# One S5 block and its SwiGLU on one core: the factor products as sums, and the first halves of the last two units ahead of the late part

## The chip, the cores and the metric

The program runs on one core of a Trainium2 chip. The core has a matrix engine (TensorE, here PE, with its weight loads PEld), a vector engine (VectorE, DVE), a scalar engine (ScalarE, ACT), a general engine (GpSimd, POOL) and a queue processor (SyncE, SP). Each takes its instructions in the order in which they are written, and waits on semaphores of the others. DMA transfers are issued by SP, ACT or POOL and run beside the engines. The metric is the time of one execution in microseconds (us) on the device.

## The reference

The function is one layer of a backbone on 1024 latent tokens and 256 context tokens with 1024 channels: a bidirectional S5 mixer (64 groups of 16 channels, 64 complex states each, two directions, the latent scan starting from the final context state), a GELU and a gated linear unit, then a SwiGLU with 2816 hidden channels. All inputs and outputs are float32.

```python
def s5_direction(u_ctx, u_lat, lam_re, lam_im, log_step, b_re, b_im, c_re, c_im):
    lam = lax.complex(lam_re.astype(F32), lam_im.astype(F32))
    lam_bar = jnp.exp(lam * jnp.exp(log_step.astype(F32))[:, None])
    b_bar = ((lam_bar - 1.0) / lam)[..., None] * lax.complex(b_re.astype(F32), b_im.astype(F32))
    ...
        _, h = lax.associative_scan(_linear_combine, (a, bu), axis=0)
        return jnp.einsum('lgn,ghn->lgh', h, c_mat).real, h[-1]
...
    def out(y, h):
        y = y.reshape(h.shape).astype(h.dtype) + d_skip * h
        g = jax.nn.gelu(y)
        return g * jax.nn.sigmoid(g @ w_glu + b_glu)
...
        x = x + m_l[2][:, None] * y_l
        h_l = modulate(rms_norm(x, norm_ffn[i]), m_l[3][:, None], m_l[4][:, None])
        x = x + m_l[5][:, None] * swiglu(h_l, ffn_w1[i], ffn_w3[i], ffn_w2[i])
    return rms_norm(x, norm_final)
```

## The kernel before, in words

**Blocks of eight steps.** The 1024 latent tokens are 128 columns of T = 8 steps. The state is scanned on DVE from column to column (`scan()`, about 97 us in one piece), for all groups and both directions at once, in a tile `STE` in RA (its quarters `STQ[0]` to `STQ[3]`). What a column adds to the output is then two products on PE: the states at its edge times a matrix `CL` (powers of lambda times C), and the block's own inputs times a Toeplitz matrix of the kernel values.

**Units.** The 64 groups are worked off as eight units of 8 groups, 0 to 7; two units share a quarter q = unit // 2 of `CL`. The columns of a unit are made in two halves, as the scan reaches the middle first: `states_mm(k, ..., 0, ...)` multiplies the first half's states into two PSUM banks and `x_mm` adds the Toeplitz product of all columns; ACT copies that to `Y`. After the scan the late half follows, and DVE adds it to `Y`. Since the second direction runs backwards, its states are copied in reversed order first (`turned`).

**Two strings set the order.** `PROG1` and `PROG2` list operations that `run` emits one by one on all engines; each engine keeps that order. A letter names the operation, its digits the unit, quarter or part:

- A: matmuls of the modulation (weights loaded by SP); M0 copies their sums out and frees a buffer. G, L, q, n: sign, load and sums for `CL`'s factors.
- C: the products of `CL` for quarter q (C20 to C23 for q = 2), five steps per direction: three products on POOL (`prod`) and two adds. `HOWS` says of each add where it runs: P on PE (two matmuls with the identity, then an ACT copy), Y as a DMA that accumulates into its target, issued by POOL (L696), E as an add on POOL.
- K: the kernel values of a unit on PE (L842 to L850), copied out of PSUM by ACT and written to DRAM (`kd`, L854 and L855). T: a Toeplitz matrix read back from `kd` by SP (L863); unit k needs T(2k) and T(2k+1), which take buffer number (index mod 4) in RA.
- R: the reversed first-half states, on ACT (L955). P: first half and transform of a unit on PE (L975, L999). Y: copies of its two banks to `Y` on ACT (L1057). F: fills of the odd columns on POOL.
- Z, N, D: reversed late states, late half on PE (L975) and its add on DVE (L1063). z, Q: for units 6 and 7 alone, reversed states of all columns, then on PE transform (L999) and states of all columns (`states_all`, L988). H: GELU on ACT, for units 6 and 7 straight from PSUM (L1069), else in place (L1066).
- I, J: transposes of four steps of a unit on PE (L1123), high parts on ACT and low parts on DVE. w, l, b, m: loads by SP. W, V: the gate's weight rounded (L1080) and its rest (V1, on POOL and DVE). x: a factor on `Y` on POOL. g: matmuls of the gated unit (L1163, L1164); g03 is token step 0 with units 0 to 3, g05 the same with unit 4 and 5. The other matmuls of that unit begin at L1175.

The first string runs while DVE scans. In the second one PE is fed by N, I, Q and g; then come the rest of the gated unit and the SwiGLU, which take the remaining three quarters of the time and aren't touched. Each T waits for all writes of its `kd` and for its buffer; each Y copy frees a PSUM bank; the late part takes its banks from the same eight.

Of the kernel before, what the change touches and what calls it, by code (L numbers as in the profile page):

```python
# [13 lines left out]
AF = mybir.ActivationFunctionType  # L14
# [3 lines left out]
P = 128  # L18
# [11 lines left out]
HOWS = "YPYP EPEP YEYE YPYE"  # L30
ZEN = "VVSVSVSV"
PROG1 = ("A22 G1 B0 A26 A30 C01 O0 C03 q1 A34 K0 O1 A38 A42 C10 C11 K1 O2 L2 A46 A50 C12 C13 A54 K2 O3 A58 T0 T1 T2 T3 F10 F11 G2 R0 K3 L3 R1 P0 Y0 Y1 A64 M0 P1 T4 T5 R2 Y2 Y3 G3 q2 C20 T6 T7 C21 P2 R3 Y4 Y5 C22 M1 P3 Y6 Y7 C23 q3 C30 K4 K5 R4 T8 T9 T10 T11 C31 C32 C33 F30 F31 P4 R5 Y8 Y9 K6 P5 Y10 Y11 K7 T12 T13 T14 T15 w0 l1 M2 m0 w1")
PROG2 = ("Z0 N0 Z1 Z2 D0 Z3 N1 D1 Z4 H0 H1 N2 D2 H2 N3 Z5 D3 H3 N4 D4 z6 z7 I0 J0 I1 J1 H4 N5 D5 I2 J2 H5 I3 J3 W0 W1 W2 W3 x0 x1 x2 x3 Q6 H6 I4 J4 Q7 I5 J5 V1 b0 w20 w21 l1 H7 g03 g13 I6 J6 g23 g05 g15 I7 J7 V2 g26 x10 x11 x12 x13")
# [9 lines left out]
def s5_ffn_kernel(tc, a, out):  # L43
# [3 lines left out]
    with ctx:  # L47
# [572 lines left out]
        def pw_sums(i):  # L620

            gs = slice(16 * i, 16 * i + 16)
            tt(PS[i], PWF[:, :, 0, :, gs], PWF[:, :, 1, :, gs], ADD, E)
            if i == 0:
                tt(PWF[:, :, 1, :, gs], PWF[:, :, 1, :, gs], PWF[:, :, 0, :, gs], SUB, E)
            else:
                for d, gs, neg in ((slice(0, 2), slice(16, 24), True), (slice(0, 1), slice(24, 32), False), (slice(1, 2), slice(24, 32), True)):
                    re, im = PWF[:, :, 0, d, gs], PWF[:, :, 1, d, gs]
                    tt(im, re if neg else im, im if neg else re, SUB, E)
# [49 lines left out]
        def cl_ops(q, d):  # L679
# [8 lines left out]
            def add(o, how, last):  # L688
                if how == "P":
                    for h in range(2):  # L690
# [3 lines left out]
                        S.activation(o[:, hs].rearrange("p g t h -> p (g t h)"), pc, AF.Copy, scale=-1.0 if last else 1.0)  # L694
                elif how == "Y":
                    E.dma_start(o, ct, accum_op=ADD)  # L696
# [1153 lines left out]
```

## Time and profile before

| what | value |
| --- | --- |
| three runs | 1011.56, 1005.89, 1008.38 us, median 1008.38 |
| profiled execution | 1006.91 us, span 1005.1 us, mean granted clock 0.984 |
| ACT busy | 427.7 us (43%) |
| DVE busy | 774.3 us (77%) |
| HBM read, written | 83.20 MB, 6.17 MB |

How to read it: the span is the time from the first to the last instruction of the profile, the execution has some microseconds around it. A row of a timeline gives the start, the busy time of the group, the engine, the line, the operation, target<-sources by the program's names, their shape (partitions x elements) and count; in square brackets is the idle time before it and what ended it. PE records two passes for a float32 matmul, so 32 matmuls of the program are 64 records. A trailing q on an engine's name means that it issues a DMA. `c` is a tile of `CL`, `pw`, `pm` and `kt` are PSUM banks of the first string, `pe` those of the second.

### The profile page before, as it was taken

The page shows a single profiled execution, that of the slowest core. Times are in us where ns is not written, and L with a number is a line of the kernel's source. Part 1 is how long each engine was busy: PE and PEld are TensorE (multiplying, and loading weights), DVE is VectorE, ACT ScalarE, POOL GpSimd, SP SyncE. Part 2 cuts the span into 40 slices and gives each one's busy share as a digit, 9 for nine tenths or more (in the row PEclk, how much of TensorE's full clock was granted, in tenths as well). Part 3 has the DMA queues.
Part 4 walks back from the last instruction along what each step waited for, and adds up shares of the span by engine and source line. Part 5 has one row for each costly group of instructions (what it writes and reads, how often), then busy time and mean ns, then how long its engine had stood idle before and what let it go on. Part 6 is the DMA issues. An engine that isn't in the chain of part 4 may idle for free. (4 is left out here: it accounts for less than half of the span.)

```text
span 1005.1 us, 17726 instructions
## 1 busy us (share of the span) xinstructions
PE 952.8 (95%) x6604; PEld 751.5 (75%) x6604; DVE 774.3 (77%) x1630; ACT 427.7 (43%) x808; POOL 748.7 (74%) x595
## 2 busy tenths in 40 slices
PE   5987898879999999999999999999999999999996
PEld 1466535769888778778888888888888888888885
DVE  7979899984556778878869586685958677686977
ACT  5478622224434563343233343434243343334337
POOL 5799998963734458979786869777785878777764
PEclk9999998889999999999999999999999999999999
DMA  9765998535520032011212121111212120111205
GB/s 335 285 133 108 287 316 273 125 85 171 210 64 22 1 105 84 11 43 42 74 53 74 42 79 34 47 61 45 74 42 84 43 64 32 61 55 53 74 22 167
DMA packets 49118, 99.95 MB, mean 99 GB/s; under 512 B 4348, under 2 KB 18940, under 8 KB 47752
## 3 DMA queue, kind: packets, MB, share of 16 engines
q1 hardware_dynamic: 43416, 86.64, 26.1%
q0 software_dynamic: 2592, 9.44, 5.1%
q10 hardware_dynamic: 3024, 2.74, 0.9%
q8 instruction: 52, 0.85, 0.3%
q14 instruction: 34, 0.28, 0.1%
HBM read 83.20 MB, written 6.17 MB: 89 GB/s over the span
## 5 line engine op out<-in xcount | busy, mean ns | idle before, releaser
L77 POOL TENSOR_TENSOR c<-rxc,c 128x512 fp32r<-128x512 f32 x127 | 166.0, 1320 | 52.3 <-ACT c L1305 51.5
L1364 PE MATMUL ut<-ra,c 128*128 128x512 f32 x400 | 155.7, 389 | 1.2 <-DVE ra L77 1.2
L1363 PE MATMUL ut<-ra,c 128*128 128x512 f32 x400 | 155.7, 389 | 0.2 <-ACT ra L1305 0.2
L1365 PE MATMUL ut<-ra,c 128*128 128x512 f32 x400 | 155.6, 389 | 0.0
L1305 ACT CAST c<-rxc 128x512 fp32r<-128x512 f32 x128 | 79.0, 622 | 147.6 <-PE xt L1658 53.0
L1658 PE MATMUL xt<-c,c 128*128 128x512 f32 x540 | 129.7, 389 | 0.0
L77 DVE TENSOR_TENSOR ru<-ru,xt 128x1024 f32<-128x1024 f32 x90 | 107.9, 1216 | 13.4 <-PE xt L1658 9.4
L1658 PEld LDWEIGHTS xt<-c,c 128*128 128x128 f32 x540 | 101.4, 188 | 21.0
L77 DVE TENSOR_TENSOR ru<-ut,ru 128x512 f32<-128x512 f32 x98 | 67.2, 686 | 44.1 <-PE ut L1365 38.6
L1364 PEld LDWEIGHTS ut<-ra,c 128*128 128x128 f32 x400 | 75.1, 188 | 17.1 <-POOL rxc L77 1.5
L1363 PEld LDWEIGHTS ut<-ra,c 128*128 128x128 f32 x400 | 75.1, 188 | 16.1 <-ACT ra L1305 0.6
L1365 PEld LDWEIGHTS ut<-ra,c 128*128 128x128 f32 x400 | 75.1, 188 | 15.6
L77 POOL TENSOR_TENSOR c<-ru,c 128x512 fp32r<-128x512 f32 (+1 forms) x39 | 58.8, 1507 | 10.1 <-ACT c L1305 5.7
L77 POOL TENSOR_TENSOR rxc<-rxc 128x512 f32<-128x512 f32 (+1 forms) x44 | 63.8, 1450 | 2.2 <-ACT rxc L671 0.6
L77 POOL TENSOR_TENSOR c<-rw,c 128x512 fp32r<-128x512 f32 (+1 forms) x28 | 37.4, 1337 | 37.5 <-ACT c L1305 37.5
L1363 PE MATMUL ut<-c,c 128*128 128x512 f32 x160 | 62.3, 390 | 0.8 <-DVE rxa L77 0.8
L1364 PE MATMUL ut<-c,c 128*128 128x512 f32 x160 | 62.3, 389 | 0.0
L1365 PE MATMUL ut<-c,c 128*128 128x512 f32 x160 | 62.2, 389 | 0.0
L1658 PE MATMUL ut<-c,c 128*128 128x512 f32 x216 | 51.9, 389 | 0.0
L77 DVE TENSOR_TENSOR ru<-ru,ut 128x512 f32<-128x512 f32 x76 | 47.3, 680 | 0.7 <-ACT ru L1712 0.5
L1658 PEld LDWEIGHTS ut<-c,c 128*128 128x128 f32 x216 | 40.5, 188 | 8.4
L587 PE MATMUL pv<-ru,c 128*64 128x160 f32 x512 | 41.4, 312 | 5.2 <-ACT c L450 2.0
(453 smaller groups left out, 2392.0 us busy)
## 6 DMA issues: line engine op xcount, KB each, us to landing
c<-in_ada_w SPq DMA_DIRECT2D x46, 256.0 KB, 5.9
rxc<-in_w SPq DMA_DIRECT2D x38, 256.0 KB, 2.9
rxc<-in_w SPq DMA_DIRECT2D x19, 512.0 KB
c<-c POOLq DMA_DIRECT2D x11, 512.0 KB, 5.7
ru<-in_w SPq DMA_DIRECT2D x11, 512.0 KB
rw<-in_w SPq DMA_DIRECT2D x11, 512.0 KB, 3.6
ra<-in_ada_w SPq DMA_DIRECT2D x10, 512.0 KB, 10.8
ra<-in_ada_w SPq DMA_DIRECT2D x18, 256.0 KB, 8.8
```

The lines of the kernel that those rows point to most:

```text
L77: eng.tensor_tensor(out=o, in0=x, in1=y, op=op)
L587: PE.matmul(pv[64 * (i % 2):64 * (i % 2) + 64, ri, c0:c0 + 160], w[:, i, 64 * ri:64 * ri + 64], U[:, 8 * b + 4 * j + i], start=True, stop= ...
L1305: S.copy(o[0], x)
L1363: PE.matmul(pu, wh, bh, start=start, stop=False)
L1364: PE.matmul(pu, wh, bl, start=False, stop=False)
L1365: PE.matmul(pu, wl, bh, start=False, stop=stop)
L1658: PE.matmul(pd, w[:, cs_], b, start=j in (1, 2, 4) and n == 0, stop=n == 2, skip_group_check=j not in (1, 2, 4))
```

## The change

Of the two adds per direction of `CL` the first was a sum and the second a difference or a negated sum, which only E and P can do. Now the factors carry the sign (`pw_sums` and `cs_sum`), so that every add is a plain sum; with that the adds of quarter 2 are all accumulating DMAs (before: two DMAs, two POOL adds), and of quarter 3 the second one (before on PE). The factor sums of quarters 2 and 3 (`pw_sums(1)`, now operation n1) are two POOL operations and one on ACT, ahead of F10, where q2 had four on POOL. A64 and M0 stand before P0 now.

Units 6 and 7 are worked like the others: R6, R7, S6, S7 (first halves), X6, X7 (transforms) and Y12 to Y15 end the first string, and the second one has Z6, Z7, N6, N7, D6, D7 for z6, z7, Q6, Q7. S7 and X7 use the banks `pw` and `pm`. K7 stands right behind K6 now and w0 between T13 and T14.

```diff
@@ -27,10 +27,10 @@
 NS = 64
 EPS = 1e-6
 MAGIC = 12582912.0
-HOWS = "YPYP EPEP YEYE YPYE"
+HOWS = "YPYP EPEP YYYY YYYE"
 ZEN = "VVSVSVSV"
-PROG1 = ("A22 G1 B0 A26 A30 C01 O0 C03 q1 A34 K0 O1 A38 A42 C10 C11 K1 O2 L2 A46 A50 C12 C13 A54 K2 O3 A58 T0 T1 T2 T3 F10 F11 G2 R0 K3 L3 R1 P0 Y0 Y1 A64 M0 P1 T4 T5 R2 Y2 Y3 G3 q2 C20 T6 T7 C21 P2 R3 Y4 Y5 C22 M1 P3 Y6 Y7 C23 q3 C30 K4 K5 R4 T8 T9 T10 T11 C31 C32 C33 F30 F31 P4 R5 Y8 Y9 K6 P5 Y10 Y11 K7 T12 T13 T14 T15 w0 l1 M2 m0 w1")
-PROG2 = ("Z0 N0 Z1 Z2 D0 Z3 N1 D1 Z4 H0 H1 N2 D2 H2 N3 Z5 D3 H3 N4 D4 z6 z7 I0 J0 I1 J1 H4 N5 D5 I2 J2 H5 I3 J3 W0 W1 W2 W3 x0 x1 x2 x3 Q6 H6 I4 J4 Q7 I5 J5 V1 b0 w20 w21 l1 H7 g03 g13 I6 J6 g23 g05 g15 I7 J7 V2 g26 x10 x11 x12 x13")
+PROG1 = ("A22 G1 B0 A26 A30 C01 O0 C03 q1 A34 K0 O1 A38 A42 C10 C11 K1 O2 L2 A46 A50 C12 C13 n1 A54 K2 O3 A58 T0 T1 T2 T3 F10 F11 G2 R0 K3 L3 R1 A64 M0 P0 Y0 Y1 P1 T4 T5 R2 Y2 Y3 G3 q2 C20 T6 T7 C21 P2 R3 Y4 Y5 C22 M1 P3 Y6 Y7 C23 q3 C30 K4 K5 R4 T8 T9 T10 T11 C31 C32 C33 F30 F31 P4 R5 Y8 Y9 K6 K7 T12 T13 w0 P5 Y10 Y11 T14 T15 l1 M2 m0 w1 R6 S6 R7 S7 X6 Y12 Y13 X7 Y14 Y15")
+PROG2 = ("Z0 N0 Z1 Z2 D0 Z3 N1 D1 Z4 H0 H1 N2 D2 Z5 H2 N3 D3 Z6 H3 N4 Z7 D4 H4 I0 J0 N5 D5 I1 J1 H5 W0 W1 N6 D6 I2 J2 H6 I3 J3 W2 W3 x0 x1 x2 x3 N7 D7 I4 J4 H7 V1 b0 w20 w21 l1 I5 J5 g03 g13 I6 J6 g23 g05 g15 I7 J7 V2 g26 x10 x11 x12 x13")
 NS1, NS2 = 46, 3
 LOG2E = 1.4426950408889634
 LN2H = 0.693359375
@@ -620,13 +620,10 @@
         def pw_sums(i):
 
             gs = slice(16 * i, 16 * i + 16)
-            tt(PS[i], PWF[:, :, 0, :, gs], PWF[:, :, 1, :, gs], ADD, E)
-            if i == 0:
-                tt(PWF[:, :, 1, :, gs], PWF[:, :, 1, :, gs], PWF[:, :, 0, :, gs], SUB, E)
-            else:
-                for d, gs, neg in ((slice(0, 2), slice(16, 24), True), (slice(0, 1), slice(24, 32), False), (slice(1, 2), slice(24, 32), True)):
-                    re, im = PWF[:, :, 0, d, gs], PWF[:, :, 1, d, gs]
-                    tt(im, re if neg else im, im if neg else re, SUB, E)
+            re, im = PWF[:, :, 0, :, gs], PWF[:, :, 1, :, gs]
+            tt(PS[i], im, re, SUB, E)
+            tt(im, im, re, ADD, E)
+            S.activation(im, im, AF.Copy, scale=-1.0)
 
         def pair(hb, eng):
             b, d = bd(hb)
@@ -672,7 +669,7 @@
 
         def cs_sum(q):
             c0, c1, c2 = (Cs[q % 2][:, i].rearrange("p d g h -> p (d g h)") for i in range(3))
-            tt(c2, c0, c1, SUB, E)
+            tt(c2, c0, c1, ADD, E)
 
         MB = view(RXa, 0, [D])
 
@@ -685,20 +682,20 @@
             def prod(i, o):
                 tt(o, bc(Cs[q % 2][:, (2, 1, 0)[i], d], 2, T), bc(fac[i][:, ::1 - 2 * d].rearrange("p t a -> p a t"), 3, HC), MUL, E)
 
-            def add(o, how, last):
+            def add(o, how):
                 if how == "P":
                     for h in range(2):
                         hs, pc = slice(4 * h, 4 * h + 4), pw([512])
                         for i, src in enumerate((o, ct)):
                             PE.matmul(pc, ident, src[:, hs].rearrange("p g t h -> p (g t h)"), start=i == 0, stop=i == 1)
-                        S.activation(o[:, hs].rearrange("p g t h -> p (g t h)"), pc, AF.Copy, scale=-1.0 if last else 1.0)
+                        S.activation(o[:, hs].rearrange("p g t h -> p (g t h)"), pc, AF.Copy)
                 elif how == "Y":
                     E.dma_start(o, ct, accum_op=ADD)
                 else:
-                    tt(o, o, ct, SUB if last else ADD, E)
+                    tt(o, o, ct, ADD, E)
 
             h0, h1 = HOWS.split()[q][2 * d:2 * d + 2]
-            return [lambda: prod(0, ct), lambda: prod(1, o0), lambda: add(o0, h0, False), lambda: prod(2, o1), lambda: add(o1, h1, True)]
+            return [lambda: prod(0, ct), lambda: prod(1, o0), lambda: add(o0, h0), lambda: prod(2, o1), lambda: add(o1, h1)]
 
         PPAIR = (3, 5, 7, 8, 9, 11, 13, 14, 15)
         UACT = {1: (2, 0, 4), 2: (2, 4, 8), 3: (3, 0, 4), 4: (3, 4, 8)}
@@ -948,9 +945,8 @@
         def turned(k, half, hs, eng):
 
             e = 8 * (k % 2) + 4
-            n = 128 if half == 2 else 64
-            c1 = 94 if half == 0 else 158
-            src = STQ[k // 2][:, c1:c1 - n:-1, :, e:e + 4]
+            c1 = 158 if half else 94
+            src = STQ[k // 2][:, c1:c1 - 64:-1, :, e:e + 4]
             if eng is S:
                 S.copy(hs, src)
             else:
@@ -975,19 +971,6 @@
                             PE.matmul(flat(pts[gp][cs_, a_]), st, flat(CL[k // 2][ps, ri, d, 4 * (k % 2) + a_]),
                                       start=start and a_ + ri == 0, stop=stop and ri == 1 and a_ == 3)
 
-        def states_all(k, pts, hs):
-
-            for a_ in range(4):
-                for ri in range(2):
-                    for d in range(2):
-                        for c in range(2):
-                            cs_ = slice(64 * c, 64 * c + 64)
-                            for gp in range(2):
-                                ps = slice(64 * gp, 64 * gp + 64)
-                                st = hs[ps, cs_, ri, a_] if d else STQ[k // 2][ps, 31 + 64 * c:95 + 64 * c, ri, 8 * (k % 2) + a_]
-                                PE.matmul(flat(pts[gp][cs_, a_]), st, flat(CL[k // 2][ps, ri, d, 4 * (k % 2) + a_]),
-                                          start=False, stop=a_ + ri + d == 5)
-
         def x_mm(k, pool):
 
             new = not isinstance(pool, list)
@@ -1001,9 +984,8 @@
 
         scan()
         inner, KO = {}, {}
-        HSe = [view(r, kb, [64, 2, 4]) for r, kb in ((RC[3], 14), (RC[3], 12), (RC[3], 14), (RC[3], 12), (RA, 2), (RA, 0))]
-        HSl = [view(RA, STB * (i // 3) + 4.125 + 2 * (i % 3), [64, 2, 4]) for i in range(6)]
-        HSq = {6: view(RA, 0, [P, 2, 4]), 7: view(RA, STB, [P, 2, 4])}
+        HSe = [view(r, kb, [64, 2, 4]) for r, kb in ((RC[3], 14), (RC[3], 12), (RC[3], 14), (RC[3], 12), (RA, 2), (RA, 0), (RA, STB), (RA, STB + 2))]
+        HSl = [view(RA, STB * (i // 3) + 4.125 + 2 * (i % 3), [64, 2, 4]) for i in range(6)] + [view(RA, 2 * i, [64, 2, 4]) for i in range(2)]
 
         def run(prog):
 
@@ -1024,8 +1006,8 @@
                     cs_sign(i)
                 elif op == "q":
                     cs_sum(i)
-                    if i == 2:
-                        pw_sums(1)
+                elif op == "n":
+                    pw_sums(i)
                 elif op == "B":
                     bb_put(1, bb_turn(1))
                     bb_put(0, bb_turn(0))
@@ -1044,15 +1026,15 @@
                     turned(i, 0, HSe[i], S)
                 elif op == "Z":
                     turned(i, 1, HSl[i], ENG[ZEN[i]])
-                elif op == "z":
-                    turned(i, 2, HSq[i], ENG[ZEN[i]])
                 elif op == "P":
                     inner[i] = [pw([4, T, HC]) for _ in range(2)]
                     states_mm(i, inner[i], 0, HSe[i], True, False)
                     x_mm(i, inner[i])
-                elif op == "Q":
-                    inner[i] = x_mm(i, pe8)
-                    states_all(i, inner[i], HSq[i])
+                elif op == "S":
+                    inner[i] = [pw([4, T, HC]), pw([4, T, HC]) if i == 6 else pm.rearrange("p (a t h) -> p a t h", a=4, t=T)]
+                    states_mm(i, inner[i], 0, HSe[i], True, False)
+                elif op == "X":
+                    x_mm(i, inner[i])
                 elif op == "Y":
                     S.copy(yview(i // 2, i % 2), inner[i // 2][i % 2])
                 elif op == "N":
@@ -1062,11 +1044,7 @@
                     for gp, po in enumerate(late[i]):
                         tt(yview(i, gp), po, yview(i, gp), ADD)
                 elif op == "H":
-                    if i in late:
-                        S.activation(Y[:, i], Y[:, i], AF.Gelu_apprx_tanh)
-                    else:
-                        for gp in range(2):
-                            S.activation(yview(i, gp), inner[i][gp], AF.Gelu_apprx_tanh)
+                    S.activation(Y[:, i], Y[:, i], AF.Gelu_apprx_tanh)
                 elif op == "I":
                     if GH[0] is None:
                         GH[0] = tuple(view(region(t, 16, R32), 0, [4, 8, P]) for t in ("c1", "c0"))
```

On POOL, the beginning of quarter 2's products (`rxc` are C's factors, `rxa` the powers, `c_65` the quarter of `CL`, `c_66` a part of a tile used for the other products), before:

```order
L77 TENSOR_TENSOR rxc<-rxc 128x256
L77 TENSOR_TENSOR rxc<-rxa 128x256
L77 TENSOR_TENSOR rxa<-rxa 128x8x2x8
L77 TENSOR_TENSOR rxa<-rxa 128x8x8 x2
L77 TENSOR_TENSOR c_66<-rxc,rxa 128x1024
L77 TENSOR_TENSOR c_65<-rxc 128x1024
L696 DMA c_65<-c_66 128x1024
L77 TENSOR_TENSOR c_65<-rxc,rxa 128x1024
L77 TENSOR_TENSOR c_65<-c_65,c_66 128x1024
```

and after:

```order
L77 TENSOR_TENSOR rxc<-rxc 128x256
L77 TENSOR_TENSOR c_66<-rxc,rxa 128x1024
L77 TENSOR_TENSOR c_65<-rxc 128x1024
L693 DMA c_65<-c_66 128x1024
L77 TENSOR_TENSOR c_65<-rxc,rxa 128x1024
L693 DMA c_65<-c_66 128x1024
```

The four small sums have left this place, and the last add has become a second DMA.

On PE, the late part up to the gated unit (`c_63` to `c_66` are the quarters of `CL`; rows of L975, 32 matmuls to a unit, are late halves; L1123 are transposes, four to a group), before:

```order
L975 MATMUL pe<-c_63,ra 64x128 x64
L975 MATMUL pe<-c_64,ra 64x128 x64
L975 MATMUL pe<-c_65,ra 64x128 x32
L1123 MATMUL pe<-r_60,ru 128x128 x8
L975 MATMUL pe<-c_65,ra 64x128 x32
L1123 MATMUL pe<-r_60,ru 128x128 x8
L999 MATMUL pe<-ra,ru 128x128 x8
L988 MATMUL pe<-c_66,ra 64x128 x64
L1123 MATMUL pe<-r_60,ru 128x128 x4
L999 MATMUL pe<-ra,ru 128x128 x8
L988 MATMUL pe<-c_66,ra 64x128 x64
L1123 MATMUL pe<-r_60,ru 128x128 x4
```

and after, from the last two matmuls of X7 on:

```order
L982 MATMUL pw<-ra,ru 128x128
L982 MATMUL pm<-ra,ru 128x128
L971 MATMUL pe<-c_63,ra 64x128 x64
L971 MATMUL pe<-c_64,ra 64x128 x64
L971 MATMUL pe<-c_65,ra 64x128 x32
L1101 MATMUL pe<-r_60,ru 128x128 x4
L971 MATMUL pe<-c_65,ra 64x128 x32
L1101 MATMUL pe<-r_60,ru 128x128 x4
L971 MATMUL pe<-c_66,ra 64x128 x32
L1101 MATMUL pe<-r_60,ru 128x128 x8
L971 MATMUL pe<-c_66,ra 64x128 x32
L1101 MATMUL pe<-r_60,ru 128x128 x8
```

The transforms of units 6 and 7 stand ahead of the first late half, and of `c_66` 64 matmuls follow it where there were 128.

On SP, the last Toeplitz reads and the loads behind them (`kd_1253` before and `kd_1254` after belong to units 6 and 7), before:

```order
L863 DMA ra<-kd_1252 128x4x128 x4
L863 DMA ra<-kd_1253 128x4x128 x4
L1083 DMA rxa<-in_w_glu 128x1024
L1115 DMA rxc<-in_w_glu 128x2048
L946 DMA rxa<-mbd 128x1024
```

and after:

```order
L860 DMA ra<-kd_1253 128x4x128 x4
L860 DMA ra<-kd_1254 128x4x128 x2
L1061 DMA rxa<-in_w_glu 128x1024
L860 DMA ra<-kd_1254 128x4x128 x2
L1093 DMA rxc<-in_w_glu 128x2048
L943 DMA rxa<-mbd 128x1024
```

One load of the gate's weights has moved between the second and the third read.

## The prediction

> **What bounds the kernel now.** First the page's busy times and its 40 slices, one slice being 25.1 us.
>
> ```profile
> span 1005.1 us, 17726 instructions
> PE 952.8 (95%) x6604; PEld 751.5 (75%) x6604; DVE 774.3 (77%) x1630; ACT 427.7 (43%) x808; POOL 748.7 (74%) x595
> PE   5987898879999999999999999999999999999996
> ```
>
> PE is full from the tenth slice (226 us) to the last one; ahead of it PE has gaps. So an edit ahead of 225 us counts only by the moment at which PE can begin its unbroken stretch, and an edit in that stretch counts by the PE work it takes out. The page's chain of what ended last explains 2% of the span and helps with neither. Windows show the border (columns: length; PE, PEld, DVE, ACT and POOL busy, with counts; granted clock, DMA share, GB/s).
>
> ```profile
> 200.00:225.00 25.00, 19.52 (x491) 15.82 (x490) 21.64 (x116) 6.19 (x13) 18.51 (x23) 0.82 0.36 85
> 225.00:250.00 25.00, 24.59 (x618) 23.75 (x620) 12.22 (x20) 12.31 (x16) 8.31 (x8) 1.00 0.58 171
> ```
>
> The timeline of DVE and PE about the border, in order of time: the scan's last add, the late halves of units 0 to 5 (N0 to N5, of which most records follow on the first row), unit 6's transform (its whole states, Q6, follow at 240.7), a transpose group (I4), unit 7's transform, then the first matmul of the gated unit (g03).
>
> ```profile
> 220.82 0.29 DVE L77 TENSOR_TENSOR ra<-ltc,ra 128x128 f32<-128x128 f32 x1
> 224.97 9.27 PE L975 MATMUL pe<-c,ra 64*64 64x128 f32 x287 [0.85 <-issue]
> 238.34 1.95 PE L999 MATMUL pe<-ra,ru 128*128 128x128 f32 x16
> 244.89 0.66 PE L1123 MATMUL pe<-r,ru 128*128 128x128 f32 x4
> 245.38 1.95 PE L999 MATMUL pe<-ra,ru 128*128 128x128 f32 x16
> 251.90 0.47 PE L1163 MATMUL pe<-c,c 128*128 128x512 f32 x1
> ```
>
> The scan ends at 221.1, N0 starts at 224.97 and g03 at 251.90: 26.9 us. **The time is decided by when g03 starts**, as PE has no gap behind it.
>
> **After N0: what is removed.** A transpose group takes 0.49 (244.89 to 245.38). Up to 238.34 there stand six N and two groups: (13.37 - 0.98) / 6 = 2.06 for one N. The changed order has eight N and the same six groups ahead of g03: 8 x 2.06 + 6 x 0.49 = 19.4. So 7.5 us go, and the **break-even** is N0 at 251.9 - 19.4 = 232.5, 7.5 later than now. Do the other engines keep up? Groups by line from 225 to 265 (busy, mean ns, idle before):
>
> ```profile
> L77 DVE TENSOR_TENSOR ru<-pe,ru 128x512 f32<-128x512 f32 x12 | 7.7, 686 | 6.6 <-PE pe L975 6.5
> L77 DVE TENSOR_TENSOR c<-pe,c 128x512 fp32r<-128x512 f32 x8 | 5.4, 688 | 13.8 <-ACT c L1125 13.8
> ```
>
> A unit costs DVE two adds and a low part, 2.06, against 2.55 on PE (N and I), and ACT is busy for half of the window from 225 to 250: they keep up. One place is late: J5 now stands behind V1 on DVE (row below, 5.24). D7 begins after N7, at N0+18.5, and takes 1.4; J4 0.7, V1 5.2, J5 0.7: N0+26.5. PE reaches unit 5's piece of g05 near N0+26, so I charge **0.5**, from bounds of 0 and 1.2 (V1 with J5 a bit later).
>
> **Ahead of N0: what is added.** PE takes S6, S7, X6, X7 before N0. The cost of each is that of the same work for unit 5:
>
> ```profile
> 209.43 2.08 PE L999 MATMUL pw<-ra,ru 128*128 128x128 f32 x8 [3.55 <-DMA ra<-kd]
> 212.12 2.08 PE L999 MATMUL pw<-ra,ru 128*128 128x128 f32 x8 [0.61 <-DMA ra<-kd]
> 216.47 2.27 PE L975 MATMUL pw<-c,ra 64*64 64x128 f32 x64
> 218.67 2.05 PE L999 MATMUL pw<-ra,ru 128*128 128x128 f32 x16
> 193.66 0.36 ACT L854 COPY r<-kt 128x240 f32<-128x240 f32 x1 [1.35 <-PE pm L850]
> 197.29 0.36 ACT L854 COPY rw<-kt 128x240 f32<-128x240 f32 x1 [2.46 <-PE pm L850]
> 198.44 0.33 ACTq L855 DMA_DIRECT2D kd<-rw  x1
> 213.81 1.08 ACT L1057 COPY ru<-pw 128x512 f32<-128x512 f32 x2 [8.97 <-PE pw L999]
> 216.60 0.36 ACT L854 COPY r<-kt 128x240 f32<-128x240 f32 x1 [1.72 <-PE pm L850]
> 224.11 1.14 ACT L955 COPY ra<-ra 128x512 f32<-128x512 f32 x2 [0.54 <-ACT rw L854]
> ```
>
> A first half is 2.27 and a transform 2.05, together 8.6 for units 6 and 7. Let E be the end of unit 4's first half (P4): now 213.7, just ahead of its copies at 213.81. The new order on PE is P4 K6 K7 P5 S6 S7 X6 X7 N0. K6's first copy follows E by 2.9 (216.60), K7's that by 3.63 (the pitch of K4 and K5), and K7's matmuls end 0.4 later: E+6.9. P5 is 4.25 (216.47 to 220.72): E+11.2. Then ACT makes two copies for Y (1.08) and the reversed states R6 (half of 1.14), for which S6 waits: E+12.8. Four pieces of 8.6 make E+21.4. N0's second matmul needs a bank that Y14's copy frees, 0.2 and 0.54 later: **N0 = E + 22.2**. Break-even is thus E = 210.3.
>
> A **floor** lies under it: R6's target lies in RA between columns of the scan's state tile, and its write is ordered behind the scan's last add (221.1). With 0.6 for R6, 8.6 and 0.74, N0 can't start before 231.0, so the gain of this part is at most 1.5.
>
> **When does P4 end?** E hangs on the second Toeplitz read (T9): its transform starts at 212.12 and E is 1.6 later. The SP and POOL rows, and DMA use by the microsecond (columns: length, clock, DMA share, GB/s):
>
> ```profile
> 202.24 1.24 SPq L863 DMA_DIRECT2D ra<-kd  x2
> 201.91 0.88 POOL L696 DMA_DIRECT2D c<-rw  x1 [0.30 <-POOL c L77]
> 175.54 2.02 POOL L77 TENSOR_TENSOR c<-rxc,rxa 128x1024 f32<-128x1024 f32 x1 [2.10 <-PE pm L534]
> 187.30 2.39 POOL L77 TENSOR_TENSOR c<-c,c 128x1024 f32<-128x1024 f32 x1
> 205.00:206.00 1.00, 1.00 1.19 164
> 210.00:211.00 1.00, 0.50 0.60 142
> c<-c POOLq DMA_DIRECT2D x11, 512.0 KB, 5.7
> ```
>
> Today the accumulating DMA of C32 (201.91) runs into the reads that begin at 202.24: the share is 1.19 with both and 0.60 with reads alone. The change moves that DMA. POOL loses the wait of 2.10 at 175.54 (A64 now runs before P0), two adds such as that of 2.39 at 187.30, each replaced by an issue of 0.9, and a part of its sums, which n1 does early. That is 2.1 + 2 x 1.5 = 5.1 and a little more: C32's issue comes near 196.5 and is done by 202, by the 5.7. It then lies beside K5's writes (last issue 198.44), so I leave the start of T8 at 202.24, with bounds of 200.4 (K7's distance of 1.9, rows below) and 204 (as much later). For the reads it is a companion less: four of 256 KB and one DMA of 512 KB share the way from 202.24 to 212.12, and a third of these 9.9 us is the companion's, 3.3. T9 then lands at 208.8, with bounds of 207 (T8 at 200.4) and 212.1 (nothing gained); I take 208.8, as the shares in the rows, 1.19 and 0.60, speak for two streams that hinder each other. E = 210.4, **N0 = 232.6, 0.1 past break-even**. The added DMAs of C21 and C23 are over long before: C23's goes out near 184 and C32's first product, which overwrites its source, comes after 192.
>
> The clock comes in here. PE's wait of 3.55 at 209.43 and the windows go together:
>
> ```profile
> 208.00:212.00 4.00, 2.08 (x8) 1.78 (x8) 4.00 (x24) 0.00 (x0) 3.92 (x6) 0.64 0.60 143
> 212.00:216.00 4.00, 3.88 (x109) 3.62 (x111) 4.00 (x24) 1.08 (x2) 3.84 (x7) 0.50 0.24 71
> ```
>
> K6's 2.9 is therefore a half-clock value, and as C31's matmuls and copies are gone, PE's wait for T8 only grows; I keep 2.9 and 1.6. At full clock both would be 1.5 shorter together.
>
> The Trainium skill (TensorE: Matmul & The Clock Gate, Part 1: The HAM clock gate) says that an idle window of about 3.4 us brings half rate, and that about 3.4 us of sustained work bring it back. The trace agrees, 3.55 idle and 0.50 after; by that rule the longer wait before T8 costs nothing beyond what is in the sum, and a gap of that length ahead of N0 would cost more (a rival, below).
>
> **X7's transfers.** In the new order w0 (the gate's weights) stands between T13 and T14 on SP, and T14 must also wait for P5.
>
> ```profile
> 223.59 0.47 ACTq L855 DMA_DIRECT2D kd<-rw  x1
> 225.50 4.46 SPq L863 DMA_DIRECT2D ra<-kd  x4
> 230.02 1.90 SPq L1083 DMA_DIRECT2D rxa<-in_w_glu  x1
> 237.84 1.04 POOL L1080 CAST c<-rxa 128x1024 fp32r<-128x1024 f32 x1 [18.57 <-DMA rxa<-in_w_glu]
> 242.73 1.04 POOL L1080 CAST c<-rw 128x1024 fp32r<-128x1024 f32 x1 [3.85 <-DMA rw<-in_w_glu]
> ```
>
> K7's last write goes out 1.15 after its first copy (198.44 - 197.29), at E+7.7, and T12 1.91 later (223.59 to 225.50): E+9.6 = 220.0. Issuing five takes 4.46 + 1.90, so T15 is out by 226.4. It lands between then (at once) and 232.3 (all five as now, 225.50 to 237.84 = 12.3). X7 needs T14 at E+19.3 = 229.7 and T15 a microsecond later. The wait costs 0 to 1.6; I take **0.5**.
>
> Behind g03 the gate's split on POOL must be in time:
>
> ```profile
> 253.41 5.24 DVE L77 TENSOR_TENSOR ra<-rxc,c 128x1024 fp32r<-128x1024 f32 x2
> 254.19 3.38 POOL L77 TENSOR_TENSOR ra<-rw,c 128x1024 fp32r<-128x1024 f32 x1
> 263.86 1.98 PE L1175 MATMUL pe<-ra,c 128*128 128x512 f32 x8
> ```
>
> Now it ends at 257.6, for a use at 263.9 (12.0 behind g03). The casts W0 to W3 now need N5 done, N0+12.9, and with the present distance from W0 to the split's end, 257.6 - 237.8 = 19.8, less W1's wait of 3.9 for its data (242.73), it ends at N0+28.8; the use is at N0+31.4. It is hidden, with 2.6 to spare.
>
> **Sum.** 0.1 + 0.5 + 0.5 = +1.1 us. The profiled execution took 1006.91 (span 1005.1), so 1008.0. The median of the three runs is 1.5 above that execution, on which it would be 1009.5; I name **1008.4**, nearer the profile's.
>
> **Rivals.** (1) *The floor doesn't hold or the reads come at once.* If T8 goes out at 200.4 and T9 lands 4.1 later instead of 6.6, and R6 needn't wait for the scan, E = 206.1 and N0 = 228.3: without the two small waits the change is worth -4.2, 1002.7, and 1001.2 if the clock stays up. For it: nothing but these reads keeps PE waiting there. Against: no read here landed so fast, and the floor. With the floor it is -1.5: 1005.4.
> (2) *X7 stalls in PE's queue and the clock falls.* N0 and all late work stand behind X7, which stands behind T14 and w0. X6 ends near 229.7; if T14 lands after 233.3, 3.6 later, N0 starts after 236.0 (X7 2.05 and 0.74) and the first 4 us at half clock cost another 2: with J5, 3.5 + 2 + 0.5 = +6.0, 1012.9, and as much if T9 too is as late as now (E = 213.7, N0 = 235.9) and the gap follows from that. The deciding point is T14 at 233.3. Against: five transfers took 12.3 in all, which gives 232.3.
> The Trainium skill (the same page and section) makes such a fall a rule for gaps over 3.4 us; by it the fall comes in this rival alone.
> (3) *POOL's split becomes the bound*: decided where W0 starts after N0+15.5; price 2 at most, 1010.
> (4) *No effect*: E falls so that N0 is at 232.5, and J5 is in time: 1007.
>
> **Chances.** The forecast with (4) and the floor's version of (1): 0.58. (1) in full 0.18, (2) 0.17, (3) 0.07. 0.5% is 5.0 us, about what a measurement of this kernel can tell from no change. Faster by more: 0.18 (as the median lies 1.5 above the profile); slower by more 0.19; within 0.63. The range of 8 in 10 takes in most of (1) and (2): 1002 to 1013.
>
> **What would show it.** Right: T8 issued near 202, T9 before 210, no accumulating DMA beside the reads; R6 right behind 221; N0 at 231 to 234; g03 about 19.4 behind N0. Wrong: N0 before 230 (floor), a DMA wait over 2 us at X7 or a clock of 0.5 after it (rival 2), a PE wait at g05 over 1 us, or any gap of PE behind L1175.

## The result and the profile after

The changed kernel took 1022.35 us (median of four runs, 1020.91 to 1023.78), the one before 1008.18 (1005.89 to 1011.56): **ratio 1.014, 95% interval 1.0115 to 1.0165**, 14 us slower and outside the range. The profiled execution took 1023.78, span 1022.0 (before 1006.91 and 1005.1).

The page of the changed kernel: busy times, and PE's 40 slices, one slice now 25.6 us.

```profile
span 1022.0 us, 17721 instructions
PE 958.8 (94%) x6596; PEld 755.6 (74%) x6596; DVE 778.9 (76%) x1634; ACT 430.1 (42%) x812; POOL 746.6 (73%) x594
...
PE   5988899768999999999999999999999999999996
```

PE's busy time grew by 6.0 us and the span by 16.9, so most of the loss is waiting; PE is again full from the eleventh slice on. How PE reaches that stretch is in its timeline, read like the rows of before: unit 1's transform, unit 4's, the first and third quarters of X7 that waited, N0, g03, and the pass with unit 5.

```profile
184.74 3.50 PE L982 MATMUL pw<-ra,ru 128*128 128x128 f32 x16 [3.70 <-DMA ra<-kd]
219.30 4.02 PE L982 MATMUL pw<-ra,ru 128*128 128x128 f32 x16 [1.57 <-DMA ra<-kd]
244.69 0.49 PE L982 MATMUL pw<-ra,ru 128*128 128x128 f32 x2 [0.30 <-DMA ra<-kd]
246.60 0.49 PE L982 MATMUL pw<-ra,ru 128*128 128x128 f32 x2 [0.75 <-DMA ra<-kd]
247.69 2.78 PE L971 MATMUL pe<-c,ra 64*64 64x128 f32 x67
268.62 0.47 PE L1141 MATMUL pe<-c,c 128*128 128x512 f32 x1
276.00 0.50 PE L1142 MATMUL pe<-c,c 128*128 128x512 f32 x1 [0.47 <-DVE c L77]
```

g03 starts at 268.62 instead of 251.90: 16.7 later, as the span is 16.9 longer. So the argument about g03 holds, and **the whole loss lies ahead of it**. The scan ends at 222.3 (its last add 222.05, 0.29) against 221.1, so it isn't the scan. ACT's timeline dates the stages: the copies of P1, P3 and P4 (that is E), K7, P5, X6 and X7.

```profile
188.06 1.07 ACT L1039 COPY ru<-pw 128x512 f32<-128x512 f32 x2 [8.33 <-PE pw L982]
201.37 1.07 ACT L1039 COPY ru<-pw 128x512 f32<-128x512 f32 x2 [4.09 <-PE pw L982]
222.93 1.07 ACT L1039 COPY ru<-pw 128x512 f32<-128x512 f32 x2 [8.43 <-PE pw L982]
231.06 0.36 ACT L851 COPY rw<-kt 128x240 f32<-128x240 f32 x1 [4.17 <-PE pm L847]
236.52 1.07 ACT L1039 COPY ru<-pw 128x512 f32<-128x512 f32 x2 [4.30 <-PE pw L982]
244.21 1.07 ACT L1039 COPY ru<-pw 128x512 f32<-128x512 f32 x2 [5.58 <-PE pw L982]
247.57 0.58 ACT L1039 COPY ru<-pw 128x512 f32<-128x512 f32 x1 [2.29 <-PE pw L982]
```

The same rows of before, from its ACT timeline (P1 and P3):

```profile
181.35 1.07 ACT L1057 COPY ru<-pw 128x512 f32<-128x512 f32 x2 [3.88 <-PE pw L999]
191.23 1.07 ACT L1057 COPY ru<-pw 128x512 f32<-128x512 f32 x2 [3.94 <-PE pw L999]
```

P1 is 6.7 late, P3 10.1, E 9.1. The 16.7 us are thus two parts: 9.1 up to E, and from E to g03 45.7 instead of 38.1, another 7.6. POOL's timeline has the first part's beginning, the issues of the accumulating DMAs (C20 and C21, C22 and C23, then C32; those of C30 and C31, at 194.65 and 197.88, are left out) with the operation that G3's sign holds up; the transfers between 170 and 190 by the DMA view stand below it (after, then before).

```profile
173.50 0.89 POOL L693 DMA_DIRECT2D c<-c  x1 [0.30 <-DMA ra<-kd]
176.76 0.88 POOL L693 DMA_DIRECT2D c<-c  x1 [0.30 <-POOL c L77]
181.98 0.87 POOL L693 DMA_DIRECT2D c<-c  x1 [0.30 <-POOL c L77]
185.20 0.88 POOL L693 DMA_DIRECT2D c<-c  x1 [0.30 <-POOL c L77]
189.54 0.73 POOL L77 TENSOR_TENSOR rxc<-rxc 128x256 f32<-128x256 f32 x1 [3.46 <-ACT rxc L668]
203.09 0.88 POOL L693 DMA_DIRECT2D c<-rw  x1 [0.30 <-POOL c L77]
```

```profile
q0 software_dynamic: 523, 1.91, 49.4%
...
c<-c POOLq DMA_DIRECT2D x4, 512.0 KB, 8.0
```

```profile
q0 software_dynamic: 288, 1.05, 27.4%
...
c<-c POOLq DMA_DIRECT2D x2, 512.0 KB, 6.7
```

The queue of the accumulating DMAs takes 49% of the DMA engines' time there instead of 27%, just while T2 to T7 are read back. And POOL's saved time is spent on a new wait: the sign operation of G3 (L668) stands on ACT behind the copies of P1, and these are late, so POOL stands for 3.46 us and C32's DMA goes out at 203.09, later than before (201.91).

### The profile page after: what moved, and what is told of

It reads as the page before. It is cut to its first block, busy times and chain, and to the rows that moved or that the text cites. A ratio compares the mean times of both kernels' runs of the same rounds, so it can differ in the third digit from the quotient of the medians.

```text
span 1022.0 us, 17721 instructions
## 1 busy us (share of the span) xinstructions
PE 958.8 (94%) x6596; PEld 755.6 (74%) x6596; DVE 778.9 (76%) x1634; ACT 430.1 (42%) x812; POOL 746.6 (73%) x594
## 5 line engine op out<-in xcount | busy, mean ns | idle before, releaser
L77 POOL TENSOR_TENSOR c<-ru,c 128x512 fp32r<-128x512 f32 (+1 forms) x39 | 57.6, 1478 | 10.1 <-ACT c L1283 5.7
```

The lines of the kernel that those rows point to most:

```text
L77: eng.tensor_tensor(out=o, in0=x, in1=y, op=op)
```

## The experiments

All kernels in one table: median and ratio to the kernel before, run beside it on the same chip, with the interval; then, from one profiled execution each, the start of the copies of P3 and P4, of N0 and of g03. In these rows N0's first record counts, which before stands at 222.81, ahead of the 224.97 that the prediction took. These four times are of single executions, which vary (the runs of before went from 1003.9 to 1014.2 us, and the profiled ones lie up to 4.9 off their medians: R6 elsewhere 4.9 above, A64 back 3.6 below), so verdicts rest on the medians.

| kernel | median us | ratio (95%) | P3 | P4 | N0 | g03 |
| --- | --- | --- | --- | --- | --- | --- |
| before | 1008.18 | 1 | 191.2 | 213.8 | 222.8 | 251.9 |
| after | 1022.35 | 1.0140 (1.0115 to 1.0165) | 201.4 | 222.9 | 247.7 | 268.6 |
| front alone | 1011.75 | 1.0030 (1.0009 to 1.0051) | 201.5 | 219.5 | 229.4 | 257.3 |
| back alone | 1016.37 | 1.0078 (1.0053 to 1.0103) | 192.8 | 215.1 | 239.8 | 260.0 |
| letters of before | 1016.82 | 1.0077 (1.0050 to 1.0103) | 191.5 | 213.7 | 238.6 | 259.9 |
| A64 back | 1020.76 | 1.0120 (1.0080 to 1.0159) | 198.6 | 217.7 | 241.3 | 262.0 |
| C32 on POOL | 1005.46 | 0.9983 (0.9970 to 0.9996) | 192.3 | 210.6 | 222.4 | 252.8 |
| early sums | 1006.52 | 0.9995 (0.9978 to 1.0013) | 193.2 | 215.1 | 224.6 | 252.7 |
| q2 back | 1016.36 | 1.0090 (1.0066 to 1.0114) | 191.6 | 212.0 | 237.4 | 259.2 |
| w0 behind | 1015.71 | 1.0080 (1.0056 to 1.0103) | 191.2 | 215.2 | 238.1 | 259.2 |
| extra DMA | 1008.35 | 1.0012 (0.9993 to 1.0031) | 196.1 | 219.6 | 228.6 | 256.9 |
| few, old order | 1008.20 | 1.0010 (0.9989 to 1.0030) | 194.2 | 215.4 | 224.8 | 256.8 |
| few, new order | 1015.02 | 1.0064 (1.0037 to 1.0091) | 193.6 | 213.4 | 239.2 | 261.0 |
| few, new order, R6 elsewhere | 1017.37 | 1.0101 (1.0069 to 1.0134) | 200.8 | 221.5 | 245.9 | 267.2 |
| new order, C32 on POOL | 1013.81 | 1.0069 (1.0043 to 1.0095) | 194.2 | 213.3 | 240.5 | 262.0 |
| the same, X7 without its wait | 1009.05 | 1.0011 (0.9992 to 1.0030) | 191.7 | 212.0 | 234.0 | 255.6 |
| q2 alone | 1010.39 | 1.0037 (1.0014 to 1.0060) | 198.2 | 218.0 | 227.5 | 255.8 |
| early sums, C32 on POOL | 1006.92 | 0.9993 (0.9978 to 1.0008) | 193.1 | 213.5 | 222.6 | 252.7 |

**1. The change in halves.** Front alone has the letters, sums, n1 and A64's place of after, with the late order of before (from P4 on); back alone is the reverse. Two more take one thing of the front back in after: the letters, or A64's place.

```diff
 letters of before
-HOWS = "YPYP EPEP YYYY YYYE"
+HOWS = "YPYP EPEP YEYE YPYE"
 A64 back
-... R1 A64 M0 P0 Y0 Y1 P1 ...
+... R1 P0 Y0 Y1 A64 M0 P1 ...
```

> The kernel before with the edits of the factor products only (HOWS, sums, n1, A64 and M0 ahead of P0); the late part, K7 and w0 as before. Theory 1 (the added accumulating DMAs of quarter 2 delay the Toeplitz reads T2 to T7): P1's copies 6 us later than before, K4 11 later, P4 ends near 222 instead of 213.7, and N0, 11.3 behind it in the old order, near 234 instead of 225: +9 us, about 1017. Theory 3 (the loss comes from the pieces put ahead of N0): no loss, 1007 to 1009.

> The changed kernel with the factor products, HOWS, n1 and A64 as before, so that only units 6 and 7, K7 and w0 stand in the new order. Theory 1: P4 ends near 213.7 as before, and N0 22 to 25 later, 236 to 239 instead of the break-even of 232.5: +3.5 to +6.5, 1011.5 to 1015. Theory 3: nearly the whole loss, 1020 to 1022.

> The changed kernel with the HOWS string of before (quarter 2 with two accumulating DMAs and two POOL adds, quarter 3 with its add on PE); all else as changed. Theory 1: the reads T2 to T7 land as before, P1's copies near 182 to 184, P4's end near 214 to 216, and the time is that of back_alone within 3 us, 1011 to 1016. Theory 2 (A64 and M0 ahead of P0 delay P0 to P3): no gain, 1020 to 1023.

> The changed kernel with A64 and M0 behind P0 and its copies, as before. Theory 1: P0 about 3 us earlier, but T2 to T7 as late as now, and the time within 3 us of the changed kernel, 1019 to 1023. Theory 2: P1 to P3 come 7 to 10 us earlier, 1012 to 1015.

Front alone loses 3.5 us, back alone 8.1, and the letters alone account for 5.5 of after's loss (1022.35 to 1016.82), with P3 back at 191.5. A64's place gives 1.6, with intervals that overlap. So both halves lose by themselves; that the letters are the front's whole loss is shown by early sums below. Three expectations were missed: front alone, at 1011.75, lies between the two expectations (1017, or 1007 to 1009), and back alone and the letters of before came out 1.4 and 0.8 above their ranges.

**2. Which letters.** Early sums is front alone with the letters of before; q2 alone adds quarter 2's letters to it, and q2 back takes these two letters out of after. C32 on POOL changes one letter of the kernel before.

```diff
 q2 alone (against early sums)
-HOWS = "YPYP EPEP YEYE YPYE"
+HOWS = "YPYP EPEP YYYY YPYE"
 q2 back (against after)
-HOWS = "YPYP EPEP YYYY YYYE"
+HOWS = "YPYP EPEP YEYE YYYE"
 C32 on POOL (against before)
-HOWS = "YPYP EPEP YEYE YPYE"
+HOWS = "YPYP EPEP YEYE YPEE"
```

> The kernel before with plain sums, n1 and A64 in the new places, but the HOWS string of before and the late part of before. If the loss of front_alone (+3.5) is that of the HOWS letters: 1007 to 1009, no later than before, with POOL's wait at C21 gone and C32's DMA 2 to 3 us earlier. If the order of A64, M0 and n1 costs something: 1010 to 1012.

> early_sums (sums, n1 and A64 new, late part of before) with the quarter 2 letters YYYY, quarter 3 as before. Theory 1 (the two added accumulating DMAs of quarter 2): +3 to +4 against before, as front_alone, 1011 to 1012. Rival (the letter of quarter 3, C31's DMA for its add on PE): 1007 to 1009.

> The changed kernel with the HOWS letters of quarter 2 as before and only quarter 3 new. Theory 1 (the four accumulating DMAs of quarter 2 lie beside the reads T0 to T7): P3's copies return to 191 to 193 and the time to that of hows_back, 1015 to 1018. Rival (quarter 3's added DMA beside K5's writes and T8): P3 near 192, but P4's end 4 to 8 us later, 1019 to 1022.

> The kernel before, with one letter of HOWS changed: the accumulating DMA of C32, which runs beside the reads T8 to T11, becomes an add on POOL. My forecast's term (the reads have 3.3 us less in their way): P4 ends near 210.5 instead of 213.7, K6 follows at once, N0 near 222.5 and the time 2 to 2.5 us lower, 1005.5 to 1006.5. Rival (the reads are bound by their own issue and descriptors): P4's end within 1 us of before, and the time too.

Early sums is no slower than before, though C32's DMA goes out there only 0.9 earlier (201.03), not the 2 to 3 that were expected. Quarter 2's two added DMAs cost 6.0 in the one pair (after against q2 back) and 3.9 in the other (q2 alone against early sums, run on different chips, each beside the kernel before); by the ratios it is 5.0 and 4.2. Quarter 3's letter costs nothing beside them (q2 back is as fast as the letters of before). PE's waits between 160 and 225, in total, times and longest: q2 alone, then early sums.

```profile
PE pw L996 <- DMA ra<-kd: 6.9, 4, 3.7
```

```profile
PE pw L996 <- DMA ra<-kd: 2.5, 1, 2.5
```

And the windows from 175 to 195, where DMA share and granted clock stand ahead of the last number: q2 alone, then early sums.

```profile
175.00:185.00 10.00, 6.24 (x91) 5.62 (x90) 10.00 (x58) 1.59 (x3) 9.11 (x7) 0.86 0.95 209
185.00:195.00 10.00, 8.61 (x117) 7.71 (x120) 10.00 (x58) 3.14 (x8) 7.54 (x7) 0.80 0.77 173
```

```profile
175.00:185.00 10.00, 9.93 (x190) 9.06 (x188) 10.00 (x59) 3.74 (x8) 9.62 (x6) 1.00 0.76 189
185.00:195.00 10.00, 9.70 (x264) 8.70 (x258) 10.00 (x59) 2.32 (x6) 9.55 (x7) 1.00 0.46 94
```

With the two DMAs more, the DMA engines are at 0.95 of their time, the reads land late, PE is busy for 4.8 us less in these 20 us and its clock falls to 0.80.

C32 on POOL bears out the prediction's companion term: with that one DMA away from the reads, the copies of P4 come at 210.60 instead of 213.81, 3.2 sooner for 3.3 forecast. As T8 goes out at another time in each run, the way from T8's issue to P4's copies (E) tells more:

| kernel | C32's DMA goes out | T8 goes out | E | from T8 to E |
| --- | --- | --- | --- | --- |
| before | 201.91 | 202.24 | 213.81 | 11.6 |
| back alone | 203.15 | 203.75 | 215.14 | 11.4 |
| C32 on POOL | none | 202.89 | 210.60 | 7.7 |
| new order, C32 on POOL | none | 206.27 | 213.30 | 7.0 |
| early sums | 201.03 | 207.21 | 215.07 | 7.9 |
| after | 203.09 | 214.75 | 222.93 | 8.2 |

It is 10.9 to 11.9 us in the four kernels where C32's DMA goes out less than 0.7 ahead of T8 (w0 behind and extra DMA are the other two), and 7.0 to 9.2 in the other fourteen.

C32 on POOL is the only kernel whose interval lies below 1; its ratio is 0.17% below, under the half per cent named in the prediction. That is weak evidence of a gain: it is one of seventeen kernels compared, the same letter on top of early sums shows none, and in its own profiled execution g03 is no earlier (252.8 for 251.9). The earlier E is spent on waiting for the scan (last add of the scan, then N0):

```profile
221.96 0.29 DVE L77 TENSOR_TENSOR ra<-ltc,ra 128x128 f32<-128x128 f32 x1
...
222.40 11.57 PE L975 MATMUL pe<-c,ra 64*64 64x128 f32 x289 [3.96 <-DVE ra L77]
```

PE stands there for 3.96 us: the old order can't use an earlier E.

**3. Is it the load on the DMA engines as such?** Extra DMA adds two plain transfers of quarter 2's tile to unused memory to the kernel before; the few kernels take accumulating DMAs away (three fewer in the old order, three fewer in the new). In the few kernels the second part of quarter 2's factors has another sign than the reference's; the instructions are the same.

```diff
 extra DMA (against before)
+                    if q == 2:
+                        E.dma_start(DUM[d], ct)
 few (against before, or against back alone)
-HOWS = "YPYP EPEP YEYE YPYE"
+HOWS = "YPYP EPEP EPEP YPEE"
 few, new order, R6 elsewhere (against few, new order)
-... (RA, STB), (RA, STB + 2))]
+... (RA, 2), (RA, 0))]
```

> The kernel before, with two more DMAs of 512 KB from POOL's queue (C21's and C23's factor tile into an unused place in DRAM, behind the adds, which stay). Theory 1 (transfers beside the reads T2 to T7 are what costs): P3's copies 4 to 9 us later than 191.2, P4's end as much later or a little less, time +3 to +6, 1010.5 to 1014. Rival (it is the accumulation, or the waits for it, and not the traffic): P3 within 1.5 us, time within 2 us of before.

> The kernel before with no accumulating DMA in quarter 2 (two adds on POOL, two on PE) and one in quarter 3: HOWS EPEP and YPEE. Theory 1: T2 to T7 land earlier than before, P3's copies near 189, P4's end near 208 to 209; N0 then waits for the scan (221.1) and starts near 222.5, so the time is 2 to 3 us below before, 1004.5 to 1006, no better than c32_on_pool by more than 1. Rival (the reads have their own pace): as c32_on_pool, P3 at 191.

> back_alone with the same HOWS (EPEP, YPEE): the new order with its reads freed. P4 ends near 208.5; by my chain N0 = E + 22.2, plus the 2 to 3 us that X7 waited in back_alone: 232.5 to 234, at break-even or 1.5 behind it, with J5 0.5: 1007.5 to 1010. If the loss of back_alone were in the late part itself (DVE, ACT or POOL behind N0), it would stay at 1015 to 1016.

> few_new with the reversed first-half states of units 6 and 7 in the places of units 4 and 5, which the scan's last columns don't touch, so that R6 no longer waits for the scan's end. If the floor binds (P5 done before 221), 1 to 2 us earlier than few_new; if X7's wait for T14 and T15 binds, the same within 1 us, with a longer wait at X7.

All four missed. Extra DMA cost 0.6 us by the medians, within the noise. Its transfers went out at 185.52 and 195.82, some 9 us later than the added ones of after and behind T2 and T3. The first one did lie beside T4 to T7 (issued from 183.3 to 186.1), and PE's matmuls then waited for no read; so one plain transfer there cost nothing, but what two of them beside T2 and T3 would do, and whether accumulating matters, it doesn't tell. The few kernels gained nothing that the intervals show over before and over back alone: quarter 2's adds take PE 3.60 us twice there (from 181.44 and 194.24 in the old order), and K5's first copy comes at 203.3 instead of 197.3. Few, new order came out at the 1015 to 1016 that were expected if the loss lay behind N0; as its E was 213.4 and not 208.5, it doesn't decide that. R6 elsewhere frees R6 from the scan's tile and was no faster: R6 began at 224.5 or later in every run of the new order, so the floor never bound.

**4. The late order.** w0 behind is back alone with w0 behind T15. New order with C32 on POOL takes back alone and the good letter; in its twin, X7 takes unit 6's matrices, which are there (so unit 7's transform is not the reference's; the instructions are the same).

```diff
 w0 behind (against back alone)
-... K6 K7 T12 T13 w0 P5 Y10 Y11 T14 T15 l1 ...
+... K6 K7 T12 T13 P5 Y10 Y11 T14 T15 w0 l1 ...
 X7 without its wait
-                    kq = KQ[(2 * k + g // 4) % 4]...
+                    kq = KQ[(2 * min(k, 6) + g // 4) % 4]...
```

> back_alone with the load w0 behind T15 instead of between T13 and T14. Theory W (w0 is in the way of X7's reads): X7's wait, 3 us in back_alone, falls to 1 or less, and the time by 2 us, to 1014 to 1015. Rival (T14 and T15 wait for P5 to free their buffers, and then take their 5 to 8 us whatever is beside them): the wait falls by less than 1 us and the time is that of back_alone, 1015.5 to 1017.

> back_alone (the new order with the factor products of before) with C32's accumulating DMA made an add on POOL, as in c32_on_pool. Chain theory: P4's end E comes 3 us earlier than in back_alone, near 211 to 212, N0 follows by 25 (22.2 and X7's wait of 2.5 to 3), and the time is 2 to 3 us below back_alone: 1012.5 to 1014.5, still 5 above before, as E + 25 is 3.5 behind the break-even of 232.5 and J5 adds 0.5. Rival (N0 is bound by something that doesn't follow E, the scan or the reads T12 to T15 by themselves): the time of back_alone, 1016.

> new_c32 with unit 7's transform taken with unit 6's Toeplitz matrices, so that X7 waits for no read of its own (T14 and T15 are still read; the transform of unit 7 is not the one of the reference). Chain theory: X7 follows X6 at once, N0 = E + 22.2, and the time is 2 to 3 us below new_c32, 1010 to 1012. Rival (X7's wait hides another one behind it, such as the banks or the late part's other engines): no gain over new_c32.

> early_sums with C32's add on POOL, late part of before: the two edits that cost nothing or gain, together. If both count, 1004.5 to 1005.5, a little below c32_on_pool (ratio 0.9983); N0 can't start before the scan's end and its copy (222.4), so no more than 2.6 below before.

w0 isn't it: 0.7 us, within the noise, and X7 still waits 1.84 and 0.28. **X7's wait costs 4.8 us** (1013.81 to 1009.05), where 2 to 3 were expected. PE's timeline of the new order with C32 on POOL: X6, two quarters of X7 that wait, N0, g03.

```profile
231.92 2.26 PE L985 MATMUL pw<-ra,ru 128*128 128x128 f32 x16
236.73 0.49 PE L985 MATMUL pw<-ra,ru 128*128 128x128 f32 x2 [2.56 <-DMA ra<-kd]
...
238.51 0.79 PE L985 MATMUL pw<-ra,ru 128*128 128x128 f32 x2 [0.62 <-DMA ra<-kd]
...
262.02 0.47 PE L1144 MATMUL pe<-c,c 128*128 128x512 f32 x1
```

Its twin without the wait, N0, a wait among the late halves, and g03:

```profile
234.03 8.24 PE L974 MATMUL pe<-c,ra 64*64 64x128 f32 x257
243.76 2.26 PE L974 MATMUL pe<-c,ra 64*64 64x128 f32 x63 [1.50 <-issue]
...
255.61 0.47 PE L1144 MATMUL pe<-c,c 128*128 128x512 f32 x1
```

In the first one X7 ends 6.2 us after X6 (copies at 233.99 and 240.20), in the twin 1.8. In the twin N0 starts 22.0 behind P4's copies; the forecast's chain was 22.2. Even so the twin is 1.6 above the kernel before, within the noise, and 3.6 above C32 on POOL (1005.46): with no wait at X7 the new order is still no gain. Early sums with C32 on POOL is no better than C32 on POOL alone, and misses the 1004.5 to 1005.5 that were expected.

## Why the prediction was wrong

**The reads (E): the step that failed, "The added DMAs of C21 and C23 are over long before", and with it "I leave the start of T8 at 202.24".** They are over before T8. But they run beside T2 to T7, and I charged that nothing. It cost 3.9 to 6.0 us in medians. P1 to P3 stand in PE's queue ahead of K4, K5 and so of T8: a late read there delays T8 as well, and in the profiled after T8 went out 12.5 us behind 202.24, where my bounds were 200.4 and 204:

```profile
214.75 1.24 SPq L860 DMA_DIRECT2D ra<-kd  x2
```

E was 222.9 for a forecast of 210.4: these 12.5 us. I weighed the accumulating DMA only against the reads of T8 and T9. What links it to T8 is the way from P0's copies to P3's: 21.8 to 23.2 us in the four kernels with quarter 2's letters YYYY, 15.0 to 17.4 in all eleven with YEYE, and 18.8 to 20.9 in the three few kernels, with the adds on PE in between. Against before it is 6.3 of the 12.5 in after; 3.9 are P0's own (178.1 for 174.3; A64 stands ahead of it now), and 2.4 come between P3 and T8, which no run takes apart. On the whole g03 lies 16.7 behind: 0.1 as forecast, 12.5 at E, 2.6 from E to N0 and 1.5 from N0 on.

**"C32's issue comes near 196.5".** It came at 203.09 with the late copies of P1, as ACT's in-order queue made POOL wait 3.46; and at 199.68 with the letters of before. The working added POOL's savings up and didn't ask what POOL waits for next, and it didn't count the issue of C31's add, which stood on PE (8.4 us from C30's DMA to C32's, instead of 7.2). In after this did E no harm, as T8 went out 11.7 later still.

**"T9 then lands at 208.8", a companion less.** Right, and in after too: from T8's issue to E the forecast had 8.2 (202.24 to 210.4), and it took 8.2.

**N0 = E + 22.2.** Right without a wait at X7, in part by luck: 22.0 in the twin, but its pieces are off by up to 1.3 and even out. In after 24.8: K7's copies come 8.1 behind E for 6.5, and X7's two waits are 1.05.

**Two waits at 0.5.** J5's: 0.47 ahead of g05, as forecast. X7's: 1.05 in the profiled after, but in back alone, in w0 behind and with C32 on POOL 2.1 to 3.2, and with C32 on POOL 4.8 of time by the medians. That is the second term that was mis-sized. "I take 0.5" put T14 and T15 near the early end; in back alone T14 came 10.95 behind the first issue (225.21 to 236.16), near the late one (12.3 for all five). In the profiled pair X7 ends 4.4 later behind X6 than in the twin, and 3.2 of it are the two waits; the rest goes with the clock, which stands at 0.50 from 238 to 243: by the rows of X7 above, its records take 0.79 behind the second wait instead of 0.49.

**"8 x 2.06 + 6 x 0.49 = 19.4".** From N0 to g03 it took 20.9 in after and 21.6 in the twin. The 2.06 rests on two miscounts that cancel, which is luck. The 13.37 us held five and a half N, not six: 33 of the 320 records of N0 to N4 (64 to a unit) stand ahead of 224.97. And they held four transpose groups (of four records), not two:

```profile
222.81 1.32 PE L975 MATMUL pe<-c,ra 64*64 64x128 f32 x33 [0.47 <-ACT rw L854]
...
234.18 1.09 PE L1123 MATMUL pe<-r,ru 128*128 128x128 f32 x8
...
237.41 1.09 PE L1123 MATMUL pe<-r,ru 128*128 128x128 f32 x8
```

So one N is (13.37 - 4 x 0.49) / 5.5 = 2.07, and the 19.4 stands by the rows of before. It left out the waits put down to "issue" among the N (0.30 in after, 1.50 in the twin), and that an N between transposes takes 2.2 (before, N5 from 235.20 to 237.41; after and twin, the last three). With 20.9 to 21.6 from N0 to g03, break-even was at 230.3 to 231.0, not 232.5.

What the new order is worth at equal E follows from the table: from E to g03 38.1 before, 43.6 in the twin, 45.7 in after. The twin takes 7.5 us from behind N0 (29.1 to 21.6) and puts 13.0 ahead of it (9.0 to 22.0): the 8.6 of work, which is only moved, and 4.4 more, most of it waits (3.7 in the twin, 0.5 before). PE's waits in the twin from 212 to 235:

```profile
PE pm L850 <- issue: 2.2, 1, 2.2
PE pw L974 <- ACT ra L954: 0.5, 1, 0.5
PE pm L842 <- ACT r L854: 0.5, 1, 0.5
PE kt L842 <- ACT r L854: 0.5, 1, 0.5
```

K7 right behind K6 waits for K6's copies and for something that the profile doesn't name; S6 waits for R6. Before, P5 stood between K6 and K7, and from N0 on PE had no gap that the move could have filled.

**The rivals.** The second one named the right queue: "X7 stalls in PE's queue and the clock falls". It priced the stall from T14 at 233.3 on, 3.6 after X6; the stall came shorter, and in back alone and others the clock fell all the same (below), though not in the profiled after. Of the first rival, reads that come at once, no run showed anything: none issued T8 before 202.2, and none took less than 7.0 from T8 to E, where the rival has 5.7. The third needs a gap of PE behind g05, and in after PE is busy for 14.00 of the 14 us from 276 to 290 and all of the 50 behind them: POOL's split is hidden, as forecast. The floor never bound.

## What to carry to other kernels

A transfer that replaces a vector operation isn't free because its result is early: list the reads that are in flight while it runs, and who waits for them down the queue. Work that is moved within an engine's queue gains only what idle time takes it up; count the waits that come with it. And before a group's duration is used as a unit, count its records and those of its neighbours: here it came out right by luck.

## What the runs showed of the hardware

**PE's clock fell after gaps shorter than the one before.** In the kernel before it stood at 0.50 behind a wait of 3.55. In back alone a gap of 2.15 between X6 and X7 sufficed, and in q2 back two gaps, of 1.51 and 1.00 us with 1.2 us of work between, while 1.84 and 0.28 in w0 behind and 1.08 and 0.82 in A64 back left it at 1.00. The windows of back alone by the microsecond (busy PE second, clock third from the end):

```profile
234.00:236.00 2.00, 0.01 (x1) 0.00 (x0) 0.00 (x0) 0.89 (x2) 0.00 (x0) 1.00 0.82 217
236.00:237.00 1.00, 0.84 (x6) 0.84 (x7) 0.00 (x0) 0.00 (x0) 0.00 (x0) 0.85 0.90 336
237.00:238.00 1.00, 1.00 (x5) 0.70 (x5) 0.00 (x0) 0.00 (x0) 0.00 (x0) 0.50 0.98 403
```

The Trainium skill (TensorE: Matmul & The Clock Gate, Part 1: The HAM clock gate) speaks of an idle window of about 3.4 us and says that the window is free-running. Here 2.15 us were enough, so a length of 3.4 us is no safe bound for a gap.

**Two more accumulating DMAs of 512 KB delayed the reads in 256 KB pieces beside them.** From early sums to q2 alone the share rose from 0.76 to 0.95 (175 to 185), and the way from P0's copies to P3's from 15.0 to 21.8 us. Between 176 and 200, SP took up to 3.2 us to issue one such read in after, and at most 0.8 before. Whether it is the accumulation or the bytes stays open: the plain transfers of extra DMA went out too late for T2 and T3.

**PE's waits put down to "issue"**, which no semaphore ends, grew as well, and no run tells their cause. The longest of them from 160 to 252, after and then before:

```profile
PE pm L847 <- issue: 5.6, 3, 2.2
PE kt L847 <- issue: 2.2, 2, 1.4
```

```profile
PE kt L850 <- issue: 1.7, 1, 1.7
PE pe L975 <- issue: 0.9, 1, 0.9
```
